# Second phase of a bidirectional RWKV-7 layer: a 16x16 block inverse joined on TensorE, loads for both directions at once, products moved to GpSimd, a new issue order

## The chip, the cores and the metric

The kernel runs on one core of a Trainium2 chip. The metric is the device time of one execution in microseconds (us). PE is the matrix engine (PEld its weight loads), DVE the vector engine, ACT the scalar engine, POOL or GpSimd the general-purpose engine, and SP the queue from which all DMAs of this kernel are issued. Each engine and the SP queue work through their instructions in program order.

## The reference

One layer: RMS norm, a projection, a centred token shift, RWKV-7 time mixing in both directions, group norm with a bonus term and a gate, an output projection, a residual add and a last RMS norm, for a sequence of 4096 tokens and one of 512. The part that matters is the delta-rule scan, run once forward and once backward in time for each of 16 heads of 64 channels:

```python
def step(s, inp):
    r_t, w_t, k_t, v_t, kk_t, a_t = inp
    sa = jnp.einsum("bhvk,bhk->bhv", s, -kk_t)
    s = (s * w_t[:, :, None, :]
         + sa[..., None] * (kk_t * a_t)[:, :, None, :]
         + v_t[..., None] * k_t[:, :, None, :])
    return s, jnp.einsum("bhvk,bhk->bhv", s, r_t)
```

## The kernel before

The kernel has three phases. The first projects and shifts and writes r, k, v, the normalised kk (kb) and the low-rank inputs (ta) to DRAM. The third norms, gates and projects out. The second, which the change rewrites in part, computes the scan in chunks of 64 tokens.

The second phase goes through 72 steps D: 4 groups of four heads times 18 blocks of 256 tokens. A step handles both directions d (forward block and mirrored backward block) and both halves hf of two heads. In a step:

- The loads lt (ta, line 554), lk, lb, lr (k, kb, r: `load`, line 546, one DMA for each direction) bring a block in. Most of their tiles have one buffer.
- `stage_a` (561) makes the decay and gate factors: lw and la are low-rank matmuls (576), sn a running sum (591), e1 and e2 exponentials, al, kf, rh, kb, kk the products for alpha, k, rho and kappa on DVE. s0 to s7 (`scores`, 658) multiply them on PE, m0 to m3 (`masks`, 666) mask the scores into sc, and x0, x1 (`transp`, 670) transpose the kappa tile.
- The triangular 64x64 system of each chunk is inverted. ga0 and ga1 (`gather`, 721) write the two 32x32 diagonal blocks of each chunk's scores to DRAM; gw (`gather_w`, 740) reads half of them back as the tile w, and gb (`gather2`, 732) reads them as the tile lt, so that each partition holds one small system. The blocks E0 to E14 (`e_step`, 751) eliminate in 30 steps of two operations, blocks 6 and 12 on DVE and the others on GpSimd. S1 and S2 (766, 774) bring the inverse back through DRAM into xt. `stage_b` (803): xr transposes, g0 and g1 (812), h0 and h1 (826) join the two 32x32 blocks on PE, with ACT copies gc, gC, hc, hC between.
- `chain` (859) runs the state through the four chunks of each half, in order: a, r (PE), q (ACT copy of the shared bank rp), u (PE), v, V (ACT), z (PE), w, W (DVE: new state), y (PE, into the same bank as rp), and p, P decay the state; with ACT_DECAY at 4 all decays run on ACT. The next step needs this one's last state.
- yo stores the result.

g, h, and the transposes x0 and x1 share one PSUM bank of tag "px". The order of all this work is written by hand: each operation has a name and a time in the table ISSUE (27), counted from the start of its step, and `add` (535) places it at D times PERIOD plus that time; the whole list is sorted and issued. A step's work spreads over more than five periods, so about six steps are under way at once. Names end in the half and, in the chain, the chunk: r01 is step r of half 0, chunk 1.

On PE every float32 matmul shows as two records in the trace. Tile shapes differ by group: a and u 64x64 (rows by columns of the array), r, z and y 128x64, scores 64x128, transposes and low-rank 128x128, g and h 32x32.

## Time and profile before

| | us |
|---|---|
| median of 3 runs | 4765.63 (4748.75 to 4774.46) |
| the profiled execution | 4773.78 |
| its span, first to last instruction | 4772.0 |
| PE busy over the span | 4369.3 (92%) |
| DVE busy | 3437.4 (72%) |
| ACT busy | 2866.8 (60%) |
| GpSimd busy | 2608.6 (55%) |

The shares are means over three phases with different limits. The first phase ends near 1940 us, the second near 4295 us. The stretch from 2300 to 3900 us lies wholly inside the second. A matmul counts as busy until its result is written, so a busy PE isn't always one that could take no more. The time that an engine waits for another is listed by the views of waits; the chain of work that ended last follows the execution back from its end, at each point to what released it.

### The profile page before, as it was taken

Reading aid. Unit: us, or ns where it says so; the run is one execution under the profiler, and the core shown is the slowest. Engines: PE = TensorE matmul, PEld = TensorE weight load, DVE = VectorE, ACT = ScalarE, POOL = GpSimd, SP = SyncE. Lnnn points to the kernel's source line nnn. Section 1 sums busy time; section 2 is a strip of 40 time slices with the busy share of each in tenths; the row PEclk is TensorE's granted clock in tenths of the full one; section 3 lists DMA queues with packets and bytes.
Section 4 is the critical chain, followed back from the end, with each engine's and each line's share of the span. In section 5 each row is a group of like instructions: output and inputs, shape, how many; then the busy total and the mean of one; then the engine's idle time right before and its main releaser. Section 6 shows DMA issues by size and latency. Waiting matters only on the chain.

```text
span 4772.0 us, 133366 instructions
## 1 busy us (share of the span) xinstructions
PE 4369.3 (92%) x52005; PEld 3842.4 (81%) x52005; DVE 3437.4 (72%) x6182; ACT 2866.8 (60%) x7355; POOL 2608.6 (55%) x4904
## 2 busy tenths in 40 slices
PE   8999999999999999688888888888888888886999
PEld 8999999999999999567777777777777777765887
DVE  6666666666665566677877877777787788747998
ACT  5454445444544444478777877777887787862332
POOL 2333333333333333377777767777776777744553
PEclk9999999999999999799999999999999999998999
DMA  4433333333333333466666656656666666638885
GB/s 133 154 110 115 105 120 110 115 106 119 110 115 109 99 102 105 121 153 150 146 159 154 158 134 154 160 140 151 158 157 156 147 157 153 157 78 269 269 267 187
DMA packets 1278855, 687.51 MB, mean 144 GB/s; under 512 B 665232, under 2 KB 1242768, under 8 KB 1278224
## 3 DMA queue, kind: packets, MB, share of 16 engines
q1 hardware_dynamic: 1278224, 678.99, 52.3%
q8 instruction: 409, 6.70, 0.6%
q14 instruction: 222, 1.82, 0.1%
HBM read 457.50 MB, written 221.25 MB: 142 GB/s over the span
## 4 chain that ended last, share of the span: by engine, by line
PE 63%; ACT 14%; DVE 7%; DMA 6%; issue 5%; POOL 2%; SPq 1%; ACTq 0%; DVEq 0%; POOLq 0%
PE acc L232 10%; PE acc L234 10%; PE acc L233 10%; PE acc L1039 8%; DMA ta<-ta_d 4%; ACT uv L899 3%; PE z L576 3%; PE py L915 3%; PE pr L896 3%; PE sp L664 3%; PE py L919 2%; PE py L878 2%; PE pr L905 2%; PE tp L673 2%; DMA r<-r_d 2%
## 5 line engine op out<-in xcount | busy, mean ns | idle before, releaser
L232 PE MATMUL acc<-hh,wh 128*128 128x384 f32 x3264 | 1108.1, 340 | 0.0
L234 PE MATMUL acc<-hh,wl 128*128 128x384 f32 x3264 | 1097.1, 336 | 0.0
L233 PE MATMUL acc<-hl,wh 128*128 128x384 f32 x3264 | 1096.3, 336 | 0.0
L91 POOL TENSOR_TENSOR tm<-lt,w 128x120 f32<-128x120 f32 (+7 forms) x1872 | 818.6, 437 | 486.8 <-DVE w L91 291.1
L91 POOL TENSOR_TENSOR w<-w,tm 128x120 f32<-128x120 f32 (+7 forms) x1872 | 838.3, 448 | 146.7
L232 PEld LDWEIGHTS acc<-hh,wh 128*128 128x128 f32 x3264 | 617.4, 189 | 0.2
L233 PEld LDWEIGHTS acc<-hl,wh 128*128 128x128 f32 x3264 | 617.3, 189 | 0.0
L234 PEld LDWEIGHTS acc<-hh,wl 128*128 128x128 f32 x3264 | 616.3, 189 | 0.0
L91 POOL TENSOR_TENSOR s<-u 128x384 f32<-128x384 f32 (+2 forms) x312 | 268.9, 862 | 603.4 <-ACT u L457 436.0
L94 DVE SCALAR_TENSOR_TENSOR sn<-pr,pt,sn 128x128 f32<-128x128 f32 x1152 | 356.1, 342 | 244.1 <-ACT sn L889 123.3
L889 ACT ACTIVATE sn<-sn,pt 128x128 f32<-128x128 f32 x1120 | 436.5, 397 | 40.5 <-PE py L915 34.4
L457 ACT ACTIVATE u<-acc 128x384 f32<-128x384 f32 x408 | 198.2, 486 | 353.6 <-PE acc L234 353.5
L91 DVE TENSOR_TENSOR sc<-sp,mask 128x512 f32<-128x512 f32 x576 | 372.3, 676 | 41.6 <-PE sp L664 40.7
L664 PE MATMUL sp<-ar,bk 64*128 64x128 f32 x4608 | 384.2, 296 | 8.2 <-DVE sc L91 6.4
L899 ACT ACTIVATE uv<-pr 64x128 f32<-64x128 f32 x1152 | 310.8, 270 | 68.9 <-PE pr L896 53.3
L664 PEld LDWEIGHTS sp<-ar,bk 64*128 64x128 f32 x4608 | 302.5, 192 | 61.5 <-issue 30.6
L915 PE MATMUL py<-sn,ar 128*64 128x128 f32 x2240 | 250.6, 304 | 97.5 <-ACT rs L882 97.5
L91 POOL TENSOR_TENSOR xl<-rk,xh 128x384 fp32r<-128x384 f32 (+1 forms) x96 | 97.5, 1016 | 428.1 <-ACT xh L264 428.1
L896 PE MATMUL pr<-rs,xt 64*64 64x64 f32 x4608 | 251.3, 235 | 48.6 <-ACT rs L882 48.6
L905 PE MATMUL pr<-uv,tb 128*64 128x64 f32 x4608 | 260.1, 236 | 35.9 <-ACT uv L899 35.7
L91 DVE TENSOR_TENSOR xl<-kq,xh 128x384 fp32r<-128x384 f32 (+1 forms) x96 | 93.4, 973 | 269.7 <-ACT xh L264 269.7
L91 DVE TENSOR_TENSOR wl<-wr,wh 128x1024 fp32r<-128x1024 f32 x136 | 182.8, 1344 | 137.0 <-ACT wh L223 136.8
(163 smaller groups left out, 9979.8 us busy)
## 6 DMA issues: line engine op xcount, KB each, us to landing
wr<-in_rw_in_dram SPq DMA_DIRECT2D x136, 512.0 KB, 4.2
ta<-ta_d SPq DMA_DIRECT2D x144, 256.0 KB, 4.6
k<-k_d SPq DMA_DIRECT2D x288, 128.0 KB, 3.8
kb<-kb_d SPq DMA_DIRECT2D x288, 128.0 KB, 3.2
r<-r_d SPq DMA_DIRECT2D x288, 128.0 KB, 3.3
uv<-v_d SPq DMA_DIRECT2D x288, 128.0 KB, 3.1
y_d<-ys SPq DMA_DIRECT2D x144, 256.0 KB, 3.2
lt<-gd SPq DMA_DIRECT2D x144, 240.0 KB, 4.3
```

The source lines that it names most:

```text
L91: eng.tensor_tensor(out=out, in0=a, in1=b, op=op)
L94: DVE.scalar_tensor_tensor(out=out, in0=a, scalar=s, in1=b, op0=op0, op1=op1)
L232: PE.matmul(ps, wh[:, k, :], hh[:, k, :], start=(k == 0), stop=False)
L233: PE.matmul(ps, wh[:, k, :], hl[:, k, :], start=False, stop=False)
L234: PE.matmul(ps, wl[:, k, :], hh[:, k, :], start=False, stop=(k == KT - 1))
L664: PE.matmul(E["sp", i2][h][:, d, j, :], bk_(d, i)[hs], ar[hs, d, i, :], start=True, stop=True)
L889: ACT.activation(o, before(i)[:, d, :], AF.Copy, scale=pt)
L896: PE.matmul(up[ua[d], hs], S["xt"][ua[d], 8 * hf + 4 * h + i, :], rs[ua[d], hs], start=True, stop=True)
L899: ACT.activation(S["uv", hf][ua[d], d, (i, 3 - i)[d], :], up[ua[d]], AF.Copy)
L905: PE.matmul(zp[hs, d, hs], S["tb", hf][:, d, i, hs], S["uv", hf][:, d, (i, 3 - i)[d], hs], start=True, stop=True)
L915: PE.matmul(o[d], S["ar", hf][:, d, i, 64:128], before(i)[:, d, :], start=True, stop=False)
L1039: PE.matmul(pn[n], a[:, k, :], w[:, k, 512 * n:512 * (n + 1)], start=first, stop=last)
```

## The change

In the second phase:

- The inverse starts from 16x16 blocks. gw reads the four 16x16 diagonal blocks of each chunk; gather2 is gone. Seven blocks E0 to E6, all on GpSimd, eliminate in 14 steps. S1 writes into one of two DRAM tiles that were filled with zeros before the first step, S2 reads 32x32 blocks back as xs in one DMA. f0 (64 matmuls of 32x32 weights against 16 columns), an ACT copy fv into gx, i0 (again 64 such matmuls) and an ACT copy iv join pairs of 16x16 blocks; xq transposes once more; cA to cD on GpSimd copy the diagonal blocks into xt. g and h follow as before.
- k, kb and r are loaded for both directions in one DMA; ta's two DMAs are split the other way.
- The products rho (rh, rH) and k times kappa (kk, kK) run on GpSimd instead of DVE.
- ACT_DECAY becomes 0: the decays p of direction 0 run on DVE, those of direction 1 (P) stay on ACT.
- ISSUE is a new table. Its last entry is yo at 122.8 instead of 142.4; PERIOD stays 27.706. New places of names that the prediction speaks of: lt 0.0, lr0 4.7, kk1 29.5, kK1 30.1, s01 32.8, gw 50.0, E0 51.8, E6 64.6, S1 70.3, S2 73.0, xr 76.9, f0 79.6, fv 80.3, i0 80.9, iv 81.2, xq 82.1, g0 82.5, cA 88.0, a00 88.0, r00 90.2, u00 93.4.

The diff, with the table and the mere renamings left out:

```diff
-ON_DVE = (6, 12)
-ACT_DECAY = 4
+ON_POOL = ('kk', 'rh')
+ACT_DECAY = 0
 ISSUE = {
...
 }
...
+        gx = kpool.tile([128, 16, 32], F32, name="gx")
+        POOL.memset(gx, 0.0)
+        for q in range(0, 128, 32):
+            POOL.tensor_copy(out=gx[q:q + 32, :, 16:32],
+                             in_=ident[q:q + 32, q + 16:q + 32].unsqueeze(1).to_broadcast([32, 16, 16]))
+        wds = [dsc.tile([16, 2, 2, 32, 32], F32, name=f"wd{n}", bufs=1) for n in range(2)]
+        for w in wds:
+            nc.sync.dma_start(w.rearrange("x u b s t -> (x u b s t)").rearrange("(p c) -> p c", p=128),
+                              xts[0].rearrange("p a b -> p (a b)")[:, 0:512])
         order = []
-        EB = 15
...
+
+        def EWISE(n):
+            return POOL if n in ON_POOL else DVE
...
+        def both(D):
+
+            t = [tok(D, d) for d in range(2)]
+            return min(t), abs(t[1] - t[0]), (0, 1) if t[0] < t[1] else (1, 0)
+
+        def strided(view, dims):
+            return bass.AP(tensor=view.tensor, offset=view.offset, ap=dims)
+
         def load(D, hf, n, src):
             p = D // NQ * 2 + hf
             S = st.setdefault(D, {})
             x = lpool.tile([128, 2, 256], F32, tag=n, name=n, bufs=2 if n == "k2" else 1)
-            for d in range(2):
-                nc.sync.dma_start(x[:, d, :], src[128 * p:128 * (p + 1), tok(D, d):tok(D, d) + 256])
-            S[n, hf] = x
+            t0, gap, slot = both(D)
+            nc.sync.dma_start(x, strided(src[128 * p:128 * (p + 1), t0:t0 + 256], [[T, 128], [gap, 2], [1, 256]]))
+            S[n, hf] = [x[:, slot[d], :] for d in range(2)]
...
             def rho(d):
-                r2 = S["r2", hf].rearrange("p d (i t) -> p d i t", t=64)
+                r2 = S["r2", hf][d].rearrange("p (i t) -> p i t", t=64)
                 pp = E["pp"]
                 if d == 0:
-                    tt(DVE, kept("ar", 2, 4, 128)[:, 0, :, 64:128], r2[:, 0], pp[:, 0, :, 1:65])
+                    tt(EWISE("rh"), kept("ar", 2, 4, 128)[:, 0, :, 64:128], r2, pp[:, 0, :, 1:65])
...
-                k8 = S["k2", hf].rearrange("p d (i t) -> p d i t", t=64)
+                k8 = S["k2", hf][d].rearrange("p (i t) -> p i t", t=64)
                 if d == 0:
-                    tt(DVE, bk[:, 0, 64:576].rearrange("p (i x t) -> p i x t", x=2, t=64)[:, :, 1, :], k8[:, 0], e8[:, 0])
+                    tt(EWISE("kk"), bk[:, 0, 64:576].rearrange("p (i x t) -> p i x t", x=2, t=64)[:, :, 1, :], k8, e8[:, 0])
...
-        def gather2(D):
-            S = st[D]
-            gd = S["gd"]
-            lt = bpool.tile([128, 30, 32], F32, tag="lt", name="lt", bufs=2)
-            for c in range(2):
-                nc.sync.dma_start(lt[64 * c:64 * c + 64], gd.rearrange("u f h i b s t -> (u f h i b) s t")[:, 1:31])
-            S["lt"] = lt
+                    nc.sync.dma_start(S["gd"][8 * f:8 * f + 8, d, b].rearrange("x s t -> s x t"),
+                                      S["sc", f][q:q + 32, d, :, :, 32 * b:32 * b + 32].rearrange("s h i t -> s (h i) t"))
+
...
+        def halves(v):
+            v = v.rearrange("x u b s t -> (x u b) s t")
+            return [v[:, 16 * c:16 * c + 16, 16 * c:16 * c + 16] for c in range(2)]
 
         def gather_w(D):
             S = st[D]
-            w = bpool.tile([128, 16, 32], F32, tag="w", name="w", bufs=2)
-            S["w"] = w
-            gv = S["gd"].rearrange("u f h i b (a c) t -> (u f h i b) a c t", c=2)
-            for c in range(2):
-                nc.sync.dma_start(w[64 * c:64 * c + 64], gv[:, :, c, :])
+            S["w"] = bpool.tile([128, 16, 16], F32, tag="w", name="w", bufs=2)
+            for c, v in enumerate(halves(S["gd"])):
+                nc.sync.dma_start(S["w"][64 * c:64 * c + 64], v)
...
-            def e_step(j, eng):
-                lt, w = S["lt"], S["w"]
-                m, n = (j + 1) // 2, 31 - j
-                n_ = "tm" if eng is POOL else "td"
-                tm = bpool.tile([128, 128], F32, tag=n_, name=n_)
-                tm = tm[:, 0:m * n].rearrange("p (c t) -> p c t", t=n)
-                sh = [128, m, n]
-                tt(eng, tm, lt[:, j - 1, j + 1:32].unsqueeze(1).to_broadcast(sh), w[:, 0:m, j:j + 1].to_broadcast(sh))
-                tt(eng, w[:, 0:m, j + 1:32], w[:, 0:m, j + 1:32], tm, ALU.add)
+            def e_step(j):
+                w = S["w"]
+                n = 15 - j
+                tm = bpool.tile([128, 64], F32, tag="tm", name="tm")
+                tm = tm[:, 0:j * n].rearrange("p (s t) -> p s t", t=n)
+                sh = [128, j, n]
+                tt(POOL, tm, w[:, j:j + 1, j + 1:16].to_broadcast(sh), w[:, 0:j, j:j + 1].to_broadcast(sh))
+                tt(POOL, w[:, 0:j, j + 1:16], w[:, 0:j, j + 1:16], tm, ALU.add)
 
             def ones():
-                wf = S["w"].rearrange("p a b -> p (a b)")
-                for c in range(2):
-                    POOL.memset(wf[64 * c:64 * c + 64, c:c + 511:34], 1.0)
+                POOL.memset(S["w"].rearrange("p a b -> p (a b)")[:, 0:256:17], 1.0)
 
             def scatter1():
-                w = S["w"]
-                wd = dsc.tile([2, 16, 2, 16, 2, 32], F32, tag="wd", name="wd")
-                S["wd"] = wd
-                wv = wd.rearrange("u x b a c t -> (u x b) a c t")
-                for c in range(2):
-                    nc.sync.dma_start(wv[:, :, c, :], w[64 * c:64 * c + 64])
+                S["wd"] = wds[D % 2]
+                for c, v in enumerate(halves(S["wd"])):
+                    nc.sync.dma_start(v, S["w"][64 * c:64 * c + 64])
 
             def scatter2():
-                xt, wd = xts[D % 2], S["wd"]
-                S["xt"] = xt
-                for u in range(2):
-                    for b in range(2):
-                        q = 64 * u + 32 * b
-                        nc.sync.dma_start(xt[q:q + 32, :, 32 * b:32 * b + 32],
-                                          wd[u, :, b].rearrange("x a c t -> (a c) x t"))
+                S["xs"] = bpool.tile([128, 16, 32], F32, tag="xs", name="xs", bufs=2)
+                nc.sync.dma_start(S["xs"], S["wd"].rearrange("x u b s t -> (u b s) x t"))
 
             def e_block(b):
-                for j in range(1 + 30 * b // EB, 1 + 30 * (b + 1) // EB):
-                    e_step(j, DVE if b in ON_DVE else POOL)
-
-            for b in range(EB):
+                for j in (2 * b + 1, 2 * b + 2):
+                    e_step(j)
+
+            for b in range(7):
                 add(f"E{b}", D, e_block, b)
             add("ms", D, ones)
             add("S1", D, scatter1)
@@ -804,10 +807,41 @@
...
             def xtr():
-                x = d2.tile([128, 16, 32], F32, tag="x", name="x", bufs=1)
-                S["g"] = x
-                S["x"] = x
-                DVE.transpose(out=x, in_=S["xt"][:, :, 0:32])
+                S["x"] = d2.tile([128, 16, 32], F32, tag="x", name="x", bufs=1)
+                DVE.transpose(out=S["x"], in_=S["xs"])
+
+            def f_mm():
+                S["iv0"] = ps.tile([128, 16, 32], F32, tag="px", name="iv0")
+                for x in range(16):
+                    for d in range(2):
+                        for b in range(2):
+                            q = 64 * d + 32 * b
+                            PE.matmul(S["iv0"][q:q + 32, x, 0:16],
+                                      S["sc", x // 8][q:q + 32, d, x // 4 % 2, x % 4, 32 * b:32 * b + 32],
+                                      S["x"][q:q + 32, x, 0:16], start=True, stop=True)
+
+            def f_cp():
+                ACT.activation(gx[:, :, 0:16], S["iv0"][:, :, 0:16], AF.Copy)
+
+            def i_mm():
+                S["iv1"] = ps.tile([128, 16, 32], F32, tag="px", name="iv1")
+                for x in range(16):
+                    for q in range(0, 128, 32):
+                        PE.matmul(S["iv1"][q:q + 32, x, 0:16], gx[q:q + 32, x, :], S["xs"][q:q + 32, x, 16:32],
+                                  start=True, stop=True)
+
+            def i_cp():
+                ACT.activation(S["xs"][:, :, 16:32], S["iv1"][:, :, 0:16], AF.Copy)
+
+            def xtr2():
+                S["x"] = d2.tile([128, 16, 32], F32, tag="x", name="x", bufs=1)
+                S["g"] = S["x"]
+                DVE.transpose(out=S["x"], in_=S["xs"])
+
+            def diagonal(n):
+                q, b = 32 * n, n % 2
+                S["xt"] = xts[D % 2]
+                POOL.tensor_copy(out=S["xt"][q:q + 32, :, 32 * b:32 * b + 32], in_=S["xs"][q:q + 32])
...
                         PE.matmul(pt[q:q + 32, x, :], S["g"][q + 32:q + 64, x, :],
-                                  S["xt"][q + 32:q + 64, x, 32:64], start=True, stop=True)
+                                  S["xs"][q + 32:q + 64, x, :], start=True, stop=True)
 
             def x_cp(d):
                 q = 64 * d
+                S["xt"] = xts[D % 2]
                 ACT.activation(S["xt"][q:q + 32, :, 32:64], S["iv3"][q:q + 32], AF.Copy)
 
...
             for n, *f in (
                     ("xr", xtr),
+                    ("f0", f_mm),
+                    ("fv", f_cp),
+                    ("i0", i_mm),
+                    ("iv", i_cp),
+                    ("xq", xtr2),
+                    ("cA", diagonal, 0),
+                    ("cB", diagonal, 1),
+                    ("cC", diagonal, 2),
+                    ("cD", diagonal, 3),
...
-            add("gb", D, gather2, D)
```

## Rows read from the trace of the kernel before

**Rows 1.** Windows: busy us (instructions) of PE, PEld, DVE, ACT, GpSimd; clock, DMA

```profile
2300.00:3900.00 1600.00, 1425.60 (x27418) 1140.37 (x27418) 1245.18 (x2979) 1259.82 (x3734) 1179.86 (x2728) 0.96 0.63 152
2735.80:2741.60 5.80, 4.68 (x100) 3.48 (x92) 3.39 (x13) 4.57 (x13) 4.17 (x13) 1.00 1.02 259
2741.60:2755.20 13.60, 12.65 (x140) 10.07 (x142) 7.03 (x18) 7.16 (x22) 10.42 (x29) 0.50 0.54 124
2755.20:2768.00 12.80, 11.44 (x230) 9.45 (x232) 11.10 (x25) 9.61 (x28) 5.71 (x11) 1.00 0.25 65
```

**Rows 2.** Line 810: duration ns min/median/max, first and last start us

```profile
L810 DVE STREAM_TRANSPOSE x<-xt x72: 697/699/714, 2028.0 to 4258.4; 128x512 f32<-128x512 f32 x72
```

**Rows 3.** Waits of PE, 2300 to 3900 us: total us, times, longest

```profile
PE py L915 <- ACT rs L882: 71.4, 152, 0.7
PE pr L896 <- ACT rs L882: 34.6, 51, 0.7
PE z L576 <- DMA ta<-ta_d: 23.1, 36, 3.8
PE pr L905 <- ACT uv L899: 22.7, 89, 0.3
PE py L919 <- ACT uv L899: 9.6, 50, 0.2
```

**Rows 4.** The chain that ended last, from 2717 us: start us, us, group

```profile
2717.23 0.67 PE z L576 x4
2717.90 0.38 PE py L873 x8
2718.28 0.37 PE py L915 x4
2718.65 0.23 PE py L919 x8
...
2719.11 1.09 PE sp L664 x16
...
2720.58 0.59 PE tp L673 x4
```

**Rows 5.** Timeline of PE at 2127 us: start us, us, instructions

```profile
2126.96 1.20 PE L819 MATMUL iv<-x,sc 32*32 32x32 f32 x64
```

**Rows 6.** GpSimd groups, the first from the page, then 2300:3900 us: busy, mean ns

```profile
L91 POOL TENSOR_TENSOR s<-u 128x384 f32<-128x384 f32 (+2 forms) x312 | 268.9, 862 | 603.4 <-ACT u L457 436.0
...
L91 POOL TENSOR_TENSOR w<-w,tm 128x120 f32<-128x120 f32 x151 | 122.6, 812 | 11.8
...
L91 POOL TENSOR_TENSOR tm<-lt,w 128x30 f32<-128x30 f32 x101 | 30.7, 304 | 16.5 <-DMA lt<-gd 9.3 <-POOL w L91 0.5
...
L91 POOL TENSOR_TENSOR w<-w,tm 128x128 f32<-128x128 f32 x50 | 22.8, 456 | 3.9
```

**Rows 7.** Groups on DVE, 2300 to 3900 us: busy us, mean ns, idle before

```profile
L91 DVE TENSOR_TENSOR bk<-k,d 128x256 f32<-128x256 f32 x202 | 99.6, 532 | 0.0
...
L91 DVE TENSOR_TENSOR ar<-r,pp 128x256 f32<-128x256 f32 x201 | 94.4, 486 | 126.0 <-DMA r<-r_d 95.9 <-PE pr L896 14.4 <-ACT rs L882 6.5
...
L810 DVE STREAM_TRANSPOSE x<-xt 128x512 f32<-128x512 f32 x51 | 35.7, 699 | 0.0
...
L91 DVE TENSOR_TENSOR td<-lt,w 128x119 f32<-128x119 f32 x51 | 14.4, 283 | 1.7
```

**Rows 8.** Decays on ACT, 2300 to 3900 us: busy us, mean ns

```profile
L889 ACT ACTIVATE sn<-sn,pt 128x128 f32<-128x128 f32 x783 | 305.9, 397 | 28.6 <-PE py L915 23.4 <-DVE k L91 1.6 <-DVE bk L91 1.6
```

**Rows 9.** DMA issues of gather2, 2300 to 3900 us: KB each, us to landing

```profile
lt<-gd SPq DMA_DIRECT2D x100, 240.0 KB, 4.1
```

**Rows 10.** Elimination's products and its closing ones: durations, first and last start us

```profile
L91 POOL TENSOR_TENSOR tm<-lt,w x88: 223/380/1327, 1990.6 to 2090.0; 128x110 f32<-128x110 f32 x10, 128x120 f32<-128x120 f32 x9, 128x30 f32<-128x30 f32 x7, 128x56 f32<-128x56 f32 x7
...
L764 POOL MEMSET w<- x144: 118/123/124, 2021.5 to 4251.9; 64x16 f32 x144
```

**Rows 11.** Timeline of GpSimd at 2127 us: start us, us

```profile
2127.27 2.60 POOL L91 TENSOR_TENSOR w<-w,tm 128x120 f32<-128x120 f32 x1
```

More of the change, by code (lines that the diff above doesn't have):

```diff
@@ L556, in load_ta @@
             S["ta"] = lpool.tile([128, 2, 2, 256], F32R, tag="ta", name="ta", bufs=1)
-            for d in range(2):
-                t0 = tok(D, d)
-                nc.sync.dma_start(S["ta"][:, d].bitcast(F32), ta_d[d, :, :, t0:t0 + 256].rearrange("x p t -> p x t").bitcast(F32))
+            t0, t1 = tok(D, 0), tok(D, 1)
+            for x in range(2):
+                src = strided(ta_d[0, x, :, t0:t0 + 256], [[T, 128], [256 * T + t1 - t0, 2], [1, 256]])
+                nc.sync.dma_start(S["ta"][:, :, x, :].bitcast(F32), src.bitcast(F32))
         def stage_a(D, hf):
@@ L607, in bfac @@
                 kb = S["kb", hf]
-                stt(E["ah"][:, d, :], E["qa"][:, d, :], -1.0, kb[:, 0, :] if d == 0 else kb[:, 1, ::-1], ALU.add, ALU.mult)
+                stt(E["ah"][:, d, :], E["qa"][:, d, :], -1.0, kb[0] if d == 0 else kb[1][:, ::-1], ALU.add, ALU.mult)
             def facs(d):
@@ L646, in kap_k @@
                 e8 = E["ee"]
[L647 removed]
+                k8 = S["k2", hf][d].rearrange("p (i t) -> p i t", t=64)
                 if d == 0:
[L649 removed]
+                    tt(EWISE("kk"), bk[:, 0, 64:576].rearrange("p (i x t) -> p i x t", x=2, t=64)[:, :, 1, :], k8, e8[:, 0])
                 else:
[L651 to L652 removed]
+                    tt(EWISE("kk"), bk[:, 1, 0:512].rearrange("p (i x t) -> p i x t", x=2, t=64)[:, :, 0, :],
+                       k8[:, ::-1, :], e8[:, 1, :, ::-1])
             def bk_(d, i):
@@ L723, in gather @@
             if "gd" not in S:
-                S["gd"] = dsc.tile([2, 2, 2, 4, 2, 32, 32], F32, tag="gd", name="gd")
-            gd = S["gd"]
+                S["gd"] = dsc.tile([16, 2, 2, 32, 32], F32, tag="gd", name="gd")
             for d in range(2):
```

15 lines of the change are left out of this document (5 added, 10 removed), and 74 rows, old and new, of the table ISSUE.

## The prediction

> **What bounds the kernel now.** I read the stretch 2300 to 3900 us first, 51 steps of the second phase [rows 1]; the change touches only this phase. The transposes L810, one a step, run from 2028.0 to 4258.4: 71 intervals of 31.4 us [rows 2]. The profiled execution took 4773.8 us, 8 above the median 4765.6; sums are made against the former and 8 is taken off. A tenth of a microsecond a step is 7 us, and 0.5% of the kernel (24 us, about what its measurement can tell from no change) is 0.33 us a step.
>
> In [rows 1] PE is busy 1426 of 1600 us, ACT 1260, DVE 1245, GpSimd 1180. What PE needs is read from a stretch of the chain in which it waits for nobody [rows 4]. Eight records of 64 columns take 0.23 behind a group of the same tile shape (L919) and 0.38 behind another shape (L873): a change of shape costs 0.15. With that taken off: a, u and z 0.23, y 0.45 (0.22 and 0.23), r 0.22 as the first half of y, of the same form, one scores call a quarter of 0.94, a transpose group 0.44, a lora group 0.52, and the 64 records of g0 and g1 1.20 less 0.15, 1.05 [rows 5]. A step has 24 of the first, 8 r, 8 y, 16 scores calls, 4 transpose groups, 4 lora groups and g and h: 5.5 + 1.8 + 3.6 + 3.8 + 1.8 + 2.1 + 2.1 = 20.7. In the old issue order, sorted by time within one period, the shape changes 35 times: 5.2. PE needs 26.0 of the 31.4; **5.4 is waiting**.
>
> Where the 5.4 goes: the waits in [rows 3] hold 2.7 us a step on ACT copies (71.4 + 34.6 + 22.7 + 9.6 over 51 steps) and 0.45 on the load of ta. The clock explains another part. In 2735.8 to 2741.6 the DMA engines are full (share 1.02) while ta is awaited, and behind it the granted clock is 0.50, the lower of the two levels (1.2 GHz), for 13.6 us with 140 matmul records, 10.3 a us; in the next 12.8 us at 2.4 GHz there are 230, 18 a us [rows 1]. The mean of 0.96 means 8% of the time at the low level, each such us 43% poorer: 1.1 a step. The last 1.15 I put down to ends of matmuls in front of those waits. So PE is the nearest bound, with waits that come from the order and from late loads.
>
> **Part by part.** (1) *The inverse.* Thirty elimination steps of up to 128 elements, 26 on GpSimd and 4 on DVE, become fourteen on GpSimd of at most 56 elements. GpSimd loses 52 operations, all but nothing of its 23 us a step (1180 over 51), and gets 28 small ones at 0.30 (tm 128x30), 8.4 [rows 6]. DVE loses 8 operations at 0.28 [rows 7], and no longer stands between E5 and E7. PE gets f0 and i0: 64 matmuls of a 32x32 tile against 16 columns each, two records a matmul, 256 records. No row has 16 columns. The nearest, L819, is 64 records in 1.05 [rows 5]: 256 cost 4.2. The lower end is half, 2.1, if the columns streamed decide; the upper is the 0.23 that 8 records of 64 columns take, 0.029 each, 7.4 [rows 4]. I take 4.2, the same tile shape and the same weights to load. They are on PE's own path and nothing hides them. ACT gets two copies, not above the 0.40 of L889 [rows 8], DVE a second transpose (0.70) [rows 7], GpSimd four copies of 32x512, between the 0.30 of a small operation and the 0.86 of 128x384 [rows 6], say 0.6, 2.4.
>
> (2) *rho and k's kappa products to GpSimd.* DVE loses 4 at 0.49 and 4 at 0.53: 4.1 [rows 7]. On GpSimd 256 elements lie between 0.30 (30) and 0.86 (384): 0.65, 5.2 for eight. GpSimd comes to 8.4 + 2.4 + 5.2 = 16 against 23. Its operations stretch beside DVE's: 120 elements took 0.81 on average and 128 took 0.46 [rows 6]; even at 1.4 times it is 22, inside a step.
>
> (3) *ACT_DECAY 0.* ACT loses 8 decays at 0.40, 3.2 [rows 8]; DVE gets them, between nothing and the 0.28 of a 119-element product [rows 7], 2.2. DVE sheds 2.2 + 4.1 and gets 0.7 + 2.2: 3.4 lighter. ACT is 2.4 lighter. Neither is nearer to the bound than PE.
>
> (4) *Loads.* k, kb and r come in one issue each for both directions, six fewer a step, and gather2 is gone: two issues and 480 KB [rows 9]; S2 is one issue instead of four. SP's queue runs in order, so S2's wait for S1 to land and gw's wait for the gather now hold lr1, lb1 and uv0 instead of half the step's loads. 480 KB out of the full stretch ahead of ta is 1.9 us at the 259 GB/s of that stretch [rows 1]; I give ta's wait and the clock spells half, 0.75 of 1.55. Nothing to all of it are the ends. The two fills of wd before the first step stand on SP before wa and cost a microsecond once.
>
> (5) *Order.* I put both orders into one period and added up the PE work between a group and the one that needs its copy. Before, y00, y01 and y12 stand right behind the r whose copy of the shared bank they wait for (0 between), u10 and u11 have 0.4, u01, u13, z00 and z01 0.6; that is the 0.7 a time of [rows 3]. After, no y waits for a fresh copy and the least distances are 0.6 (u10) and 0.8 (u01), the rest 1.0 and more. So the 2.7 and the 1.15 in front should go, and I leave 0.2 of them. New waits: i0 for fv, with 0.7 of PE work between and a path as long as the 0.7 of [rows 3] plus ACT's queue; behind i0 stand r12, r03, the scores s4 to s7 and g0. 0.25 for it. g0 waits for xq with 1.85 between. Shape changes are 32 instead of 35.
>
> **Sum.** PE needs 20.7 + 4.2 + 32 x 0.15 = 29.7; waits 0.2 + 0.25 + 0.75 = 1.2; 30.9 a step, 0.5 less than before: 36 us over 71 steps. The fill: the first step's elimination lasted from 1990.6 to 2021.5, 30.9 us, with PE idle behind it [rows 10]. Twenty-eight operations at 0.38 with their gaps are 10.6; f0, fv, i0, iv and xq add 4.2 + 0.8 + 0.7 and the ends, 6.5. 14 shorter, of which I take 12. 4773.8 - 36 - 12 - 8 = 4718, 1.0% faster.
>
> **Rivals.** *A, small matmuls are cheap.* f0 and i0 use four tiles on the diagonal where g uses two; if records then cost half, 2.1 less a step: 149 us, 4569. For it: from 64 to 32 columns a record fell from 0.029 to 0.016 us [rows 4, 5]. Against it: there the weights shrank with the moving side; here they stay 32 columns wide, as L819's.
> The Trainium skill's page TensorEngine Tiling (Array Packing), Key Properties, says that different tiles load and multiply in parallel, which would be this case; no row here shows four tiles in use.
>
> *B, slower: the scores wait for GpSimd.* rho and kappa-k now stand in GpSimd's order behind elimination blocks and copies; PE's scores follow in order and hold the state chain behind them (r00 and z13 behind s01 to s31, u02 behind s10 to s20). Place: L664 waiting for GpSimd. It decides once kk1 and kK1, behind E0 to E2 and cD, end after PE has reached s01. A block of steps beside DVE's products costs the 0.35 between 0.81 and 0.46 an operation [rows 6]; six such ahead of each half's scores are 2.1, twice a step 4.2, less about 2 that lie between the groups in the two orders: 33.1 a step, 1.7 above before, 4773.8 + 121 - 12 - 8 = 4875. For it: DVE's four products L91 and L94 in a row, in the middle of which one GpSimd operation took 2.60 [rows 11]. Against it: GpSimd has 9 us a step to spare, and DVE has 8 such products fewer.
> The Trainium skill's page SBUF — State Buffer, section SBUF: two separate sides, says that GpSimd and a DVE operation with two SBUF inputs shut each other out for a whole instruction, in either direction. The 2.60 agrees, and by it each moved product could also hold DVE up for its own 0.65, 5.2 a step at most, more than the 4.1 that DVE sheds.
>
> *C, slower: PE's waits stay.* If filling PE only moves its waits, 3 to 5.4 of them remain: 32.7 to 35.1, 4846 to 5016.
> *D, the clock.* f0 and i0 are long and thin; a fall as in 2741.6 in every third step costs 13.6 x 0.43 / 3 = 1.9 a step, 32.8, 4853. Against it: L819 brings none in the steady stretch.
>
> **Chances.** Forecast, 4660 to 4775: 0.42. A 0.24. B 0.13. C 0.14. D 0.07. The range reaches to A's 4569 and past B and D into C: 4570 to 4900. Faster by over 0.5% (below 4742): A and over half of the forecast's span, 0.48; within 0.5%, the rest of that span and the mildest of C, 0.21; slower 0.31.
>
> **What would show it.** PE's waits for ACT copies gone from the list and f0, i0 as rows of about 2.1 us each (right); rows of 1 us (A); L664 idle for GpSimd (B); the same total of PE waits under other names (C); granted clock below 0.95 in the steady stretch (D). GpSimd at 16 to 22 us a step, ta's wait halved, first xr some 14 us sooner after the first load. The prediction is wrong if PE isn't the engine that sets 31 us: then a DVE lighter by 3.4 and an ACT lighter by 2.4 show up as steps shorter by as much.

## The result, and the profile after

The changed kernel takes 4941.9 us (median of four runs) where the kernel before took 4770.1 beside it: 1.036 times as long, 95% interval 1.030 to 1.041. The prediction said 4718, with 4570 to 4900 as its range: the result lies above it, and on the slower side. The profiled execution of after took 4945.3.

I read the period first, as in [rows 2]: line 811 is the first transpose of a step. Its row gives durations, then the first and last start in us.

```profile
L811 DVE STREAM_TRANSPOSE x<-xs x72: 700/702/712, 2010.5 to 4421.6; 128x512 f32<-128x512 f32 x72
```

The first stands 17.5 us sooner than in [rows 2], but 71 intervals take 2411 us: **33.96 us a step in place of 31.4**, 181 us in all. So the loss sits in the steady steps. The same stretch as in [rows 1] (PE, PEld, DVE, ACT, GpSimd; clock, DMA share, GB/s), 47.1 steps now:

```profile
2300.00:3900.00 1600.00, 1425.07 (x37391) 1253.86 (x37384) 1009.44 (x2436) 1090.72 (x3181) 805.81 (x1915) 0.85 0.50 121
```

DVE, ACT and GpSimd are all lighter a step than before (21.4, 23.2 and 17.1 us); the granted clock fell from 0.96 to 0.85. What PE waits for in that stretch (total us, times, longest), to be held against [rows 3]:

```profile
PE iv L830 <- issue: 120.1, 47, 6.3
PE iv L819 <- issue: 22.8, 13, 2.9
PE py L917 <- issue: 16.7, 6, 3.2
PE py L917 <- ACT ys L969: 5.2, 22, 0.2
PE sp L684 <- issue: 3.7, 4, 2.0
PE py L922 <- issue: 2.8, 2, 1.6
```

Every wait of [rows 3], for ACT's copies and for ta, is gone. In their place PE stands for "issue": for nothing that the profile shows. It does so 166 us in all, 3.5 a step (3.8 if such a gap is counted from the start of one record to the start of the next), mostly at L830, that is in the middle of i0. One such place, PE's timeline (start us, us, group):

```profile
2525.98 1.26 PE L819 MATMUL iv<-x,sc 32*32 32x16 f32 x108
2528.55 0.36 PE L819 MATMUL iv<-x,sc 32*32 32x16 f32 x20 [1.31 <-issue]
2528.84 0.68 PE L917 MATMUL py<-uv,sc 64*64 64x64 f32 x16
2529.46 0.96 PE L830 MATMUL iv<-xs,gx 32*32 32x16 f32 x92
2536.68 0.72 PE L830 MATMUL iv<-xs,gx 32*32 32x16 f32 x36 [6.27 <-issue]
```

f0 and i0 are 128 records each, and run at 10 to 12 ns a record. Here f0 breaks off after 108 and i0 after 92 (f0 breaks off in 13 of the 47 steps, i0 in every one), and the profile shows nothing that they wait for: the holes have no releaser, and they fall inside a group. What arrives during the second hole is in the DMA queues of these windows (packets, MB, share of 16 engines): none of queue q8 in 2526.3 to 2534.0 beyond the one that began just ahead of it, and this in 2534.0 to 2535.2:

```profile
q8 instruction: 1, 0.02, 5.9%
```

q8 carries instructions. On the page of before it has this row, 409 packets:

```profile
q8 instruction: 409, 6.70, 0.6%
```

and on the page of after this one, 554:

```profile
q8 instruction: 554, 9.08, 0.7%
```

That is 16 KB a packet. After has 140,874 matmul and weight-load records, 254 for each of its 554 packets: a packet is a block of about 256 TensorE instructions, and f0 and i0 (64 matmuls, each two records and two weight loads) are one block each. By the packets' times in the trace, the fetch in the example began at 2534.04 and had landed at 2535.17; PE went on 1.51 later. Of the 71 holes over 0.8 us (from start to start) in 2300 to 3900, **all 71 end 1.2 to 1.8 us after a block has landed**. Before has no such hole in the same stretch, only two waits of 0.4 us for issue; of its 89 gaps over 0.8 us, which all have a releaser, 8 end 1.1 to 1.95 us after a block.

A count of records settles where the holes stand. At each of the 71, the number of matmul and weight-load records that TensorE has begun is 254.4 times the number of blocks landed by the hole's end, plus one constant for all, to within 3 records. So every hole stands where the last landed block is used up, whatever operation that falls into. Counted the same way, at most 2.1 blocks are ahead of TensorE anywhere in the stretch: two blocks of dense small matmuls use up all that is there.

Behind the hole of 6.27 us the granted clock is at the lower of its two levels (1.2 GHz). The two windows are a stretch right behind it and a later one:

```profile
2536.80:2540.00 3.20, 3.20 (x58) 2.83 (x60) 1.35 (x3) 1.37 (x5) 0.61 (x1) 0.50 0.02 6
2541.20:2545.00 3.80, 3.71 (x124) 3.29 (x124) 2.25 (x6) 3.20 (x9) 3.56 (x7) 1.00 0.26 73
```

By the trace's clock records the level falls 47 times between 2300 and 3900 us, and all 47 falls lie inside one of the 71 holes or less than 2 us behind its end, which together is a fifth of the time. (In the example it fell at 2530.5, 1.9 us behind the first hole and at the start of the second.)

### The profile page after: what moved, and what is told of

It reads as the page before. It is cut to its first block, busy times and chain, and to the rows that moved or that the text cites. A ratio compares the mean times of both kernels' runs of the same rounds, so it can differ in the third digit from the quotient of the medians.

```text
span 4943.5 us, 167390 instructions
## 1 busy us (share of the span) xinstructions
PE 4526.9 (92%) x70437; PEld 4136.3 (84%) x70437; DVE 3216.5 (65%) x5678; ACT 2746.0 (56%) x6923; POOL 2190.0 (44%) x3973
## 4 chain that ended last, share of the span: by engine, by line
PE 48%; issue 6%; ACT 3%; POOL 2%; DVE 1%; DMA 0%; SPq 0%; ACTq 0%; POOLq 0%; DVEq 0%
PE sp L684 8%; PE acc L1082 7%; PE py L922 4%; PE z L596 3%; PE pr L949 3%; PE py L917 3%; PE tp L693 3%; PE py L959 3%; PE pr L940 3%; PE py L963 3%; PE iv L830 3%; PE iv L819 2%; PE iv L853 2%; PE iv L867 1%; PE tp L1068 1%
## 5 line engine op out<-in xcount | busy, mean ns | idle before, releaser
L94 DVE SCALAR_TENSOR_TENSOR sn<-pr,pt,sn 128x128 f32<-128x128 f32 x1152 | 365.3, 343 | 281.6 <-PE pr L949 179.5
L91 POOL TENSOR_TENSOR bk<-k,d 128x256 f32<-128x256 f32 x288 | 226.4, 796 | 486.6 <-PE py L922 185.1
L684 PE MATMUL sp<-ar,bk 64*128 64x128 f32 x4608 | 409.9, 326 | 9.3 <-issue 5.1
L684 PEld LDWEIGHTS sp<-ar,bk 64*128 64x128 f32 x4608 | 346.0, 224 | 56.4 <-issue 41.5
L91 POOL TENSOR_TENSOR w<-w,tm 128x14 f32<-128x14 f32 (+6 forms) x1008 | 330.6, 328 | 78.9
L91 POOL TENSOR_TENSOR ar<-r,pp 128x256 f32<-128x256 f32 x288 | 215.9, 770 | 303.2 <-ACT pp L616 164.1
L91 POOL TENSOR_TENSOR tm<-w 128x14 f32<-128x14 f32 (+6 forms) x1008 | 297.9, 296 | 92.5 <-DMA w<-gd 24.2
L844 POOL COPY xt<-xs 32x512 f32<-32x512 f32 x288 | 175.3, 609 | 280.1 <-issue 244.4
L917 PE MATMUL py<-uv,sc 64*64 64x64 f32 x4608 | 260.6, 240 | 34.6 <-issue 25.4
L830 PE MATMUL iv<-xs,gx 32*32 32x16 f32 x9216 | 128.4, 194 | 177.9 <-issue 177.3
L969 ACT ACTIVATE ys<-py 128x128 f32<-128x128 f32 x576 | 142.0, 274 | 251.2 <-PE py L917 238.8
```

Of the source, the lines that this page charges most:

```text
L91: eng.tensor_tensor(out=out, in0=a, in1=b, op=op)
L94: DVE.scalar_tensor_tensor(out=out, in0=a, scalar=s, in1=b, op0=op0, op1=op1)
L684: PE.matmul(E["sp", i2][h][:, d, j, :], bk_(d, i)[hs], ar[hs, d, i, :], start=True, stop=True)
L830: PE.matmul(S["iv1"][q:q + 32, x, 0:16], gx[q:q + 32, x, :], S["xs"][q:q + 32, x, 16:32], start=True, stop=True)
L917: PE.matmul(rp[ua[d], hs], S["sc", hf][va[d], d, h, i, 0:64], S["uv", hf][va[d], d, (i, 3 - i)[d], hs], start=(h == 0), stop=False)
```

## Experiments

Theory 1 is that TensorE runs out of instructions: f0 and i0 use them up faster than blocks come (1a in later expectations, where 1b is that their mere number costs, wherever they stand). Against it: the time of small matmuls as such (2), thin matmuls that lower the clock (3), another part of the change (4). All times have a run of before beside them; ratios are to it, with the 95% interval. Holes are idle time of PE put down to "issue" in 2300 to 3900 us.

**The same columns in fewer instructions.** In f0, and likewise in i0:

```diff
-                for x in range(16):
+                for x in range(0, 16, 8):
...
-                            PE.matmul(S["iv0"][q:q + 32, x, 0:16],
+                            PE.matmul(S["iv0"][q:q + 32, x:x + 8, 0:16],
```

> Kernel: the changed kernel, in which f0 and i0 take one weight load and one matmul for eight blocks (moving operand 8x16 columns wide) where there was one for each block. The columns that stream through TensorE are as many as before, the instructions of the two fall from 512 to 64 a step; the blocks two to eight get the weights of the first, so the inverse is left out in truth. Theory 1 (TensorE runs out of instructions in the dense pair f0, i0): the holes without a releaser, 3.8 us a step, go, and the clock comes back with them; 28.5 to 30 us a step instead of 34.0, 4590 to 4680 us. Theory 2 (the time of the small products themselves): f0 and i0 are busy for 2.6 us a step and stream the same columns, so 0 to 1 us a step is saved, 4870 to 4942 us. Theory 3 (thin products lower the clock): the products stay 32 rows thin, the clock stays near 0.92, 4850 to 4942 us. Theory 4 (another part of the change: loads, GpSimd's products, the new order): no change, 4900 to 4945 us.

4470.8 us, 0.930 [0.925, 0.935]; 27.33 us a step. This run and the next, with pairs, are probes and not kernels to use: blocks that differ share one block's weights. The transposes and the window:

```profile
L811 DVE STREAM_TRANSPOSE x<-xs x72: 699/703/714, 2008.9 to 3949.3; 128x512 f32<-128x512 f32 x72
```

```profile
2300.00:3900.00 1600.00, 1525.95 (x33564) 1308.33 (x33562) 1289.80 (x3032) 1356.34 (x3966) 1021.84 (x2383) 0.97 0.62 148
```

Of PE's waits, the longest and the first put down to issue:

```profile
PE py L922 <- DVE sn L94: 50.3, 53, 2.8
...
PE iv L867 <- issue: 3.3, 4, 2.2
```

The holes are all but gone (0.1 us a step) and the clock is back at 0.97. The gain, 6.6 us a step, is larger than expected. The rows of f0 and i0 in the same stretch, after and here:

```profile
L830 PE MATMUL iv<-xs,gx 32*32 32x16 f32 x6016 | 84.8, 195 | 120.3 <-issue 120.1
L819 PE MATMUL iv<-x,sc 32*32 32x16 f32 x6016 | 63.2, 180 | 22.9 <-issue 22.8
```

```profile
L830 PE MATMUL iv<-xs,gx 32*32 32x128 f32 x928 | 37.1, 274 | 0.0
L819 PE MATMUL iv<-x,sc 32*32 32x128 f32 x928 | 37.1, 274 | 0.3 <-ACT qa L603 0.3
```

They take 1.27 a step here (over 58.5 steps) and 3.14 after (over 47.1), which is 1.9 of the gain. The holes are 3.4 less, and new waits, that for DVE's state (L94) above all, take back 1.0. The 2.3 that are left are time in which PE is busy with other work, and the clock is the nearest cause: a scores matmul (L684) lasts 291 ns on average here and 325 after. 2, 3 and 4 fall as the main cause. Weight loads fell together with the matmuls in this run; the pair of runs with equal work, below, holds them equal. The run with pairs (`range(0, 16, 2)` and `x:x + 2`) is the point between:

> Kernel: the changed kernel with one weight load and one matmul for two blocks each in f0 and i0, 256 instructions a step in place of 512, at the same places and with the same columns; the second block of a pair gets the weights of the first, so the inverse is left out. Between the changed kernel (512: 34.0 us a step, 3.8 us of holes) and the eightfold one (64: 27.3, none). Theory 1a: the pair f0, i0 is one block of 256 instructions and g and h are another, and the holes fall by more than half, to 0 to 1.5 us a step; 28 to 30.5 us a step, 4520 to 4700 us. If the time goes with the matmuls' own pace and not with the fetch: half way, 4700 to 4720 us, with no holes at issue.

4566.2 us, 0.953 [0.950, 0.955], 28.7 us a step, and the holes (78 us over 55.8 steps) are 1.4 a step:

```profile
PE iv L830 <- issue: 32.9, 17, 3.2
PE iv L853 <- issue: 20.4, 20, 2.7
PE sp L684 <- issue: 9.9, 7, 2.3
PE pr L940 <- issue: 7.7, 6, 2.2
```

512, 256 and 64 instructions give 3.5, 1.4 and 0.1 us of holes a step. Halving takes away well over half of the loss. The holes also move behind i0, into g0 and the scores, and the count of records holds here too: at all 46 over 0.8 us it is 254.1 times the blocks landed plus a constant, to within 3. They stand where a block ends, not at an operation.

**The instructions alone, added to the kernel before.** 128 matmuls of f0's shape on constants, ahead of g0 in one run, then in sixteen runs:

```diff
+        def more(n):
+            for _ in range(n):
+                for q in range(0, 128, 32):
+                    PE.matmul(scratch[q:q + 32, 0:16], ident[q:q + 32, 0:32], ident[q:q + 32, 0:16], start=True, stop=True)
+        for D in range(ND):
+            order.append((D * PERIOD + ISSUE["g0"] - 0.0003, more, (32,)))
```

> Kernel: the kernel before with 128 added matmuls of 32x32 by 16 columns (512 instructions) in one run ahead of g0 in every step, on constants, into a spare corner of a PSUM tile, so that nothing waits for them but TensorE itself. Theory 1 (instruction supply): their busy time, 2.6 us a step by f0 and i0 in the trace after, and holes of 3 to 5 us a step without a releaser; part of it beside TensorE's old waits; 4980 to 5250 us, the profile with one or two holes over 0.8 us in every step in or right behind them. Theory 2 (time of the small products): up to 2.6 us a step, no holes, 4850 to 4955 us. Theory 3 (thin products lower the clock): no holes, the granted clock below 0.93 in the second phase, 4870 to 5000 us. Theory 4: below 4955 us with neither.

5342.8 us, 1.111 [1.105, 1.117], above the range: 39.28 us a step, 7.9 more than before, with the holes in the added run and right behind it (L820 is g), and the clock of the stretch at 0.86. The transposes, and PE's waits for issue:

```profile
L811 DVE STREAM_TRANSPOSE x<-xt x72: 697/699/712, 2030.5 to 4819.0; 128x512 f32<-128x512 f32 x72
```

```profile
PE pr L965 <- issue: 108.1, 48, 3.2
PE iv L820 <- issue: 33.3, 20, 2.6
```

> Kernel: the kernel before with the same 128 added matmuls a step, but in sixteen runs of 8 matmuls (32 instructions) spread evenly over the step's order. Theory 1 (it is the density that starves TensorE): no holes over 0.8 us without a releaser, though the instructions are as many as in the dense kernel; busy time of 2.6 us and some drains between tile shapes, part of it in TensorE's old waits; 4800 to 4980 us, at least 80 us under the dense one. If the mere count of instructions is the cost, it is as slow as the dense kernel, within 40 us. Theory 2 (time of the small products): as the dense kernel or above it, for the 32 more changes of tile shape a step. Theory 3 (thin products lower the clock): as the dense kernel.

5291.9 us, 1.100 [1.094, 1.106]. It is 51 us under the packed run, between the bounds of the two readings. The row of its added matmuls has no holes, but another wait, which I had put in. The spare corner shared a PSUM tile with u, so the added runs stood for ScalarE's copies (last part of the row):

```profile
L965 PE MATMUL pr<-ident 32*32 32x16 f32 x10576 | 212.4, 185 | 112.9 <-ACT uv L900 96.1 <-DVE sn L94 16.8
```

So it tells nothing on density. Again, in eight runs of 64 instructions, each ahead of a group that takes the same PSUM tag anyway:

```diff
+            scratch = ps.tile([128, 512], F32, tag=tag, name="kw")
...
+            for at, tag in (("lw0", "pl"), ("la0", "pl"), ("lw1", "pl"), ("la1", "pl"),
+                            ("x01", "px"), ("g0", "px"), ("h0", "px"), ("s51", "pa")):
+                order.append((D * PERIOD + ISSUE[at] - 0.0003, more, (tag, 4)))
```

> Kernel: the kernel before with the 128 added matmuls of 32x32 by 16 columns a step in eight runs of 16 matmuls (64 instructions), each just ahead of a group that takes the same PSUM tag anyway (lw, la of both halves, x01, g0, h0, s51), so that they bring no wait of their own; in the sixteen runs of the earlier kernel they shared a tile with u, and TensorE waited for ScalarE's copies of it, 2.4 us a step. Theory 1a (density starves TensorE): no holes over 0.8 us without a releaser; 2.8 us a step of busy time and 1 to 2 of drains between shapes, part of it in TensorE's old waits; 34 to 36.5 us a step, 4930 to 5130 us, at least 150 us under the dense kernel's 5343. Theory 1b (the count of instructions costs, wherever they stand): within 60 us of the dense kernel.

4952.8 us, 1.033 [1.032, 1.035]; 33.66 us a step, 390 us under the run with the same matmuls in one place. The transposes, the window, and the first of PE's waits put down to issue:

```profile
L810 DVE STREAM_TRANSPOSE x<-xt x72: 697/698/714, 2034.4 to 4424.5; 128x512 f32<-128x512 f32 x72
```

```profile
2300.00:3900.00 1600.00, 1446.61 (x37637) 1173.33 (x37640) 1160.42 (x2777) 1174.94 (x3483) 1111.37 (x2542) 0.98 0.59 143
```

```profile
PE kw L965 <- issue: 3.8, 6, 1.6
```

That is the cleanest pair: equal work and equal count, weight loads included, 7.9 us a step packed and 2.2 spread. They differ in one thing more, the PSUM tile: the packed run writes beside u, but its list of waits has none of the added run for ACT or DVE. The clock is 0.98 with all the thin matmuls in, so thin matmuls as such don't lower it (theory 3).

The last of the four puts the time without the count ahead of g0: 48 matmuls of 128x128 by 128 columns, `more` with `PE.matmul(scratch, warm[:, 0:128], warm[:, 0:128])`.

> Kernel: the kernel before with 48 added matmuls of 128x128 by 128 columns in bfloat16 (96 instructions) in one run ahead of g0 in every step: about the TensorE time of the 128 small ones, with a fifth of the instructions. Theory 1: no holes without a releaser; up to 2.6 us a step less what falls into TensorE's old waits, 4790 to 4955 us, at least 80 us under the dense kernel. Theory 2 (TensorE's time as such): equal to the dense kernel within 40 us. Theory 3 (thin products lower the clock): here the clock stays at or above the 0.967 of the kernel before, and the time is under that of both kernels with small products.

4924.3 us, 1.023 [1.017, 1.030]: 136 us of PE in the stretch, 2.9 a step, cost 2.1 a step and bring no holes (0.5 us in all). So TensorE's time as such costs no more than itself in this kernel; the other 5.8 of the packed run are not time of the engine.

**Parts undone**, on the eightfold kernel: `ON_POOL = ()`, `ACT_DECAY = 4`.

> Kernel: the kernel with f0 and i0 in eightfold matmuls (no holes, 27.3 us a step, 4471 us; the inverse is left out), with two other parts of the change undone: rho and the kappa products of k back on VectorE, all decays back on ScalarE. By the rows of that kernel: VectorE 22.2 us a step, plus 8 products of 0.43, less 7.8 decays of 0.38, is 22.7; ScalarE 23.4 plus 7.8 of 0.40 is 26.5 of 27.3; GpSimd 17.6 less 8 of 0.70 is 12. If these parts carry the gain that is left when the holes are gone: ScalarE ends last, 28 to 30 us a step, 4520 to 4660 us. If they don't: within 30 us of 4471.

4476.2 us, 0.933 [0.930, 0.935], the same 27.33 us a step. With the holes gone, GpSimd's products and the decays on DVE neither gain nor lose; my row sum put ScalarE at the end, and at 1482 of 1600 us it still doesn't set the step.

**The whole inverse, spread.** First by delay: f0 and i0 in four runs each and all behind them 5 units of the table ISSUE later; the control has the delay alone.

> Kernel: the changed kernel with f0 and i0 cut into four runs each of 16 matmuls (64 instructions), set about one unit of the order apart, other work between most of them, and all that follows them in a step 5 units later (x01 and what hangs on it moved out of their way). Theory 1a (density starves TensorE): the holes without a releaser fall from 3.8 us a step to below 1.5 and the clock comes up from 0.85 in the stretch; 30.5 to 32.5 us a step, 4700 to 4840 us. Theory 1b (count): as the kernel with the same delay and both uncut, within 40 us. If the later place of the chain costs more than the holes: above 4942 us, with new waits of TensorE for a releaser.

> Kernel: the same delay of 5 units, but f0 and i0 in one run each: the control for the kernel with four. Theory 1a: the holes stay, 3 to 4 us a step, fewer if the 3.8 units between f0 and i0 leave time for the fetch; 33 to 35 us a step, 4870 to 5010 us. Theory 1b: as the kernel with four runs, within 40 us.

5428.2 (1.134) and 5205.5 (1.086). Both lie far above what theory 1a gave, and the one with four runs is the slower by 223 us, the wrong way round for it; the first came out as the third case of its expectation. With 3.8 units between f0 and i0 the control has lost nearly all its holes in i0 (the last row), but in both PE stands for copies that it did not wait for before. The holes are 0.4 us a step with four runs and 0.7 in the control, so the order costs more than they do, and the two are no test of density. PE's waits with four runs each:

```profile
PE iv L859 <- DVE x L845: 56.9, 39, 1.6
PE iv L824 <- ACT tb L700: 31.5, 39, 0.8
```

and in the control:

```profile
PE pr L944 <- ACT rs L930: 57.3, 42, 1.4
...
PE iv L834 <- issue: 9.4, 8, 2.3
```

Then i0 with two blocks on the diagonal of one weight tile:

```diff
-        gx = kpool.tile([128, 16, 32], F32, name="gx")
+        gx = kpool.tile([128, 16, 64], F32, name="gx")
...
-                    for q in range(0, 128, 32):
+                    for q in range(0, 128, 64):
```

> Kernel: the changed kernel with i0 as 32 matmuls of 64 rows by 64 columns in place of 64 of 32x32: gx holds the two blocks of a pair on its diagonal and zeros beside them, and fv is four copies of 32 rows in place of one of 128 rows. The same inverse; 384 instructions in f0 and i0 instead of 512. Theory 1: a quarter of the instructions of the dense stretch go; by the eightfold kernel's 471 us for 448 instructions 128 are worth up to 135 us, and the holes fall by one fetch in some steps; 4790 to 4900 us. Theory 2 (time of the matmuls themselves): two ScalarE copies more on the path of fv, 0 to 0.5 us saved on TensorE; 4910 to 4990 us.

4913.4 us, 1.025 [1.024, 1.027]: above the range of theory 1 and at the foot of that of theory 2, a gain of 29 us on the changed kernel's median. Theory 2 has no place for the fall of the holes, to about 1.3 us a step; but i0 now stands for the four copies of fv: "PE iv L831 <- ACT gx L825" 41.2 us, 41 times. So the next step moved the front of the inverse ahead instead, f0 nine units ahead of i0, the chain left where it was:

```diff
+ISSUE.update(gw=46.97, E0=48.83, E1=49.72, E2=51.36, E3=54.8, E4=54.98, E5=55.3, E6=58.0, ms=60.9, S1=63.9, S2=66.6,
+             xr=70.6, f0=71.2, f1=72.9, fv=73.4, i0=80.0, i1=81.0, iv=81.3)
```

> Kernel: the changed kernel with the front of the second phase's inverse moved ahead (gw by 3 units of the order, the last eliminations, the scatters and xr by 6.3), so that f0 stands some 9 units ahead of i0 instead of 1.3, and with f0 and i0 in two runs each of 32 matmuls (128 instructions) with other work of TensorE between; the chain behind i0 stays where it is. All 512 instructions a step are kept and the inverse is the reference's. Theory 1a (density starves TensorE): holes without a releaser from 3.8 us a step to 1 or less, the clock of the stretch 2300 to 3900 back from 0.85 to 0.94 or more, 28.5 to 31 us a step, 4555 to 4735 us. Theory 1b (count): no gain, 4900 to 4990 us. If GpSimd can't keep the earlier places: TensorE waits for xr at f0, up to 3 us a step, 4750 to 4950 us.

> Kernel: the kernel with the early front and f0 and i0 in two runs each, and i0 as 32 matmuls of 64 by 64 (384 instructions a step in place of 512; fv in four copies of 32 rows, which now have 6 units of the order until i0). Theory 1a: as the early kernel or up to 1.5 us a step better, the ScalarE copies being off TensorE's path; 4500 to 4735 us. If ScalarE is near its limit by then (0.9 us more a step): up to 40 us slower than the early kernel.

4914.2 (1.022 [1.018, 1.026]) and 4837.1 (1.008 [1.005, 1.011]). The first came out as the third case of its expectation, the second above its range; in both, f0 now stood for its data. The row of the second:

```profile
PE iv L822 <- DVE x L813: 75.3, 38, 3.1
PE iv L822 <- issue: 18.7, 16, 1.6
```

f0 began 145 to 147 ns after xr had ended in every step of the stretch. Two attempts put f0 1.3 to 1.8 units later and x00, c00, x10 behind it; the second also set GpSimd's copies behind the elimination.

> Kernel: the kernel with the early front, f0 and i0 in two runs and i0 of 64 by 64 (32.4 us a step, 4837 us), with f0 put 1.3 to 1.8 units later, x00 and x10 of the first half pushed behind it, and gw, the eliminations and the scatters placed to match. In the trace of the former kernel f0 begins 146 ns after the end of xr in nearly every step, behind 1 to 3 us in which TensorE stands for it: that wait is late data, not instructions. Theory 1a: with the data there in time, 1.5 to 2.3 us a step go and few holes come; 29.8 to 31.2 us a step, 4650 to 4760 us, below the kernel before. If the count of instructions is what is left: above 4800 us, with holes in f0 and i0 in place of the wait for xr.

> Kernel: as the last one, and GpSimd's copies cC, cB and cA of the step before come behind the end of the elimination in place of ahead of its last steps, so that xs lands up to 1.8 us sooner. If xr is still what f0 waits for: up to 1.5 us a step faster than the last one, 4570 to 4720 us. If the copies are then late for u00: TensorE waits for GpSimd at L941, slower than the last one by up to 100 us.

5032.9 (1.051) and 5016.6 (1.047): misses. Holes were all but gone and the wait for xr fell to 18.7 and 9.8 us, but ACT's copies took its place: in the first, 87.7 us for ys at L924 and 66.2 for rs at L947 (91.9 and 67.1 in the second). I put that down to the moved transposes; f0's later place was not tried alone. Taken from the other end, with x00 and x10 back in place (`ms=58.1, S1=63.6, S2=65.1`), and then xr ahead of kf0 (`xr=70.05, f0=71.5`):

> Kernel: the early kernel with i0 of 64 by 64 (32.4 us a step, 4837 us) as it was, but GpSimd sets the ones and so ends the elimination ahead of its copies cC, cB and cA (in the trace the last elimination ends at 2518.7 and the ones come at 2521.5 us), and the two scatters are issued to match. x00 and x10 stay where they were, since moving them brought new waits of ScalarE's ys and rs. f0 stood 1 to 3 us a step for xr in that kernel; the data should now come 2 to 2.8 us sooner. Theory 1a: 30.0 to 31.2 us a step, 4660 to 4760 us, faster than the kernel before. If the order of the chain is the bound instead: 4800 to 4840 us with other waits in the place of that for xr.

> Kernel: as the last one (4774 us, 31.4 us a step), with xr half a unit of the order earlier on VectorE, ahead of kf0 (in the trace xs had landed at 2517.6 and xr began at 2518.7, behind kf0 and a state update), and f0 0.3 units later, behind u01. f0 stood 1.0 us for xr in nearly every step there. Theory 1a: that 1.0 us goes, the holes stay at 0.7 us a step; 30.3 to 30.8 us a step, 4695 to 4735 us, faster than the kernel before by 1 to 2 in a hundred. If xr so early delays ScalarE's and GpSimd's work behind kf0: 4750 to 4800 us.

4774.3, 0.995 [0.993, 0.997], just above its range, and 4751.7, **0.990 [0.988, 0.992]**, 17 us above its first range and at the foot of the second. The last is 1.0% under the kernel before, and under the changed one, with the reference's inverse kept whole and all other parts of the change in it. Its PE waits, 51.3 steps:

```profile
PE pr L947 <- ACT rs L933: 28.4, 39, 0.9
PE py L924 <- ACT ys L976: 26.5, 47, 3.0
PE iv L822 <- issue: 17.6, 17, 1.6
PE iv L822 <- DVE x L813: 15.6, 18, 1.7
```

Holes are down to 0.5 us a step. It is not at 27.3, and I did not find what the rest would take: f0 and i0 still cost their 384 instructions, and each move of the order by hand brought waits in another place.

## Why the prediction was wrong

- **The bound** was right: PE. In the eightfold kernel it is busy 26.1 of 27.33 us a step.
- **Parts 4 and 5, the loads and the order**, held: the waits for the copies and for ta are gone from after's list (ta's is 3.4 us over 58.5 steps in the eightfold kernel, where half of 0.45 a step was left in the sum), and L684 never waits for GpSimd (rival B is out). How much of it is the order, and how much the loads or the shorter elimination, was not separated. Take f0 and i0 from the forecast's 30.9 a step and 26.7 is left; take their rows from the eightfold kernel's 27.33 and 26.06 is left. All other terms together were 0.6 a step too dear.
- **Parts 2 and 3** held: "neither is nearer to the bound than PE". Undoing them in the eightfold kernel changed nothing. GpSimd came to 17.1 us a step against 16 to 22.
- **Part 1 is the step that failed**: "256 cost 4.2.", to which it adds: "They are on PE's own path and nothing hides them." In records it was too dear: 10 to 12 ns a record where I took 16, so about 2.6 in one run, between the forecast and rival A's half; as rows, f0 and i0 came to 1.3 and 1.8 a step. The Trainium skill's page TensorEngine Tiling (Array Packing), Key Properties, named for A, says that different tiles load and multiply in parallel; the cheaper record does not contradict it, but the columns fell from 32 to 16 as well, and no run parts the two. But 4.2 was meant to be the whole price, and the price measured against the eightfold kernel is 6.6 a step on top of the 1.27 left there: 7.9, above even the 7.4 that I had as upper end. Of it, 3.1 are the rows and 3.4 TensorE standing for instructions, a term that the sum did not have; 2.3 are other work of PE at the lower clock (the cause argued above), and 1.0 comes off for other waits, which only the eightfold kernel has. I priced records by the pace of a neighbour in the trace (64 records in 1.20) that is too short to use up a block; 512 instructions in some 3 us have no such row in before.
- **Rival D** had the right sign in the profile (0.85, below the 0.95 that it named) and not the cause: it put the clock down to long thin matmuls, but with as many spread it is 0.98, and all 47 falls come with a hole.
- **Rival C** held the time (4846 to 5016), and its sign came out too: PE is idle 174.4 us of the 1600 before and 174.9 after, under other names. That is luck: C meant the old waits, moved by a fuller PE, and in the eightfold kernel PE is fuller still (1526 us) and idle for 74.
- **The fill** was near: 17.5 us sooner, where 14 were worked out and 12 taken.
- No rival had instructions as a resource. The profile's page would have let me ask: 409 packets of 16 KB are in before's list of queues, 216 of them in the 1600 us of [rows 1], one in 7.4 us; 512 instructions more are two blocks a step, both within 3 us.

## What to carry to other kernels

Count TensorE's instructions in a dense stretch, not only its time: in these runs, from 2300 to 3900 us, no two blocks of about 256 were fetched less than 3.2 us apart, some two at most lay ready in the three runs counted, and a run that uses one up in 1.3 us stops. Put wide matmuls where small ones share their weights (here they don't), or set the small ones between long work; check that the place brings no wait of its own, since here a delay by hand cost more than the holes. When a change's cost is taken from a short neighbour, ask what the longer run uses up that the neighbour doesn't.

## What the runs showed of the hardware

- TensorE stops when its landed blocks of 254 records are used up: at all 71 holes of after, 46 of the pairs and 71 of the packed run the count of records fits to within 3. At most 2.1 blocks lay ahead of it in any of the three, and it goes on 1.1 to 1.8 us after the next has landed.
- Starts of two instruction blocks are never closer than 3.2 to 3.4 us in that stretch (3.32 after, 3.22 in the packed run, 3.31 eightfold; none of the 18 traces has less than 3.2), with a block's own transfer at 1.0 us (median, after). The 256 instructions of an f0 that isn't broken off ran in 1.3 us (34 of the 47 in after).
- The Trainium skill's page Runtime: NRT & Kernel Launch, section Instruction fetch mechanics, has the refill in blocks of 16 KiB, as the trace does, and calls it mostly hidden, since the sequencer dispatches more slowly than blocks come. Here it isn't: 3.5 us a step stand open.
- Most holes are longer with more DMA beside them. In after, a mean of 2.65 us where the DMA engines were busy 0.75 or more in the 3 us ahead of the fetch (53 holes), 2.2 below that (18); in the packed run 1.69 below 0.25 (26), 2.35 between 0.25 and 0.5 (14), 2.69 between 0.5 and 0.75 (30), and a single one of 0.83 above. The block's own transfer is no longer with more DMA (1.08 us against 1.10 in after). That the fetch queues behind data is argued from this; it wasn't tried.
- The granted clock fell 47 times in 1600 us of after, each time inside a hole or less than 2 us behind one; with as many thin matmuls spread it fell 6 times.
- A small matmul of four tiles in turn costs 10 to 12 ns a record at 16 columns, against 16 to 19 for g's 32 columns on two tiles ([rows 5]).
